# Output projection of a hybrid decoder layer: one fp32 product replaced by three products of hi and lo parts, with GpSimd making the weights' lo parts

## The chip, the cores and the metric

The kernel runs on one core of a Trainium2 chip. The metric is the device time of one execution in microseconds (us). Before the change the median of three runs is 924.68 us (923.85 to 926.58).

## What is computed

One decoder layer on 256 tokens of width 1024, batch 1, depth 1, float32 throughout. `c` is one vector that conditions the layer; everything between the input and the second normalization hangs on the modulation `mod`, six vectors of 1024:

```python
mod = jnp.einsum('bd,de->be', jax.nn.silu(c), w_ada[l]) + b_ada[l]
sh1, sc1, g1, sh2, sc2, g2 = jnp.split(mod[:, None, :], N_MOD, axis=-1)
h = rmsnorm(x, norm1_g[l]) * (1.0 + sc1) + sh1
proj = jnp.einsum('bsd,de->bse', h, w_in[l])
q, k, v, u = jnp.split(proj, [A, 2 * A, 3 * A], axis=-1)
attn = dilated_attention(q.reshape(B, S, N_HEADS, HEAD_DIM),
                         k.reshape(B, S, N_HEADS, HEAD_DIM),
                         v.reshape(B, S, N_HEADS, HEAD_DIM)).reshape(B, S, A)
pool = multiscale_pool(u, pool_w[l], pool_scale[l])
mixed = jnp.einsum('bse,ed->bsd', jnp.concatenate([attn, pool], axis=-1), w_out[l])
x = x + g1 * mixed
h2 = rmsnorm(x, norm2_g[l]) * (1.0 + sc2) + sh2
x = x + g2 * peer_ffn(h2, peer_wq[l], peer_subkeys[l], peer_u[l], peer_v[l])
return rmsnorm(x, final_g)
```

Attention has 8 heads of 64, the pooling mixer 4 groups of 128 channels. `peer_ffn` scores 16384 experts by product keys, takes the best 16 of each of 8 heads, and adds up their gated outputs. `mixed` is the output projection that the change touches: a 256 x 1024 by 1024 x 1024 product.

## The kernel before

Everything is held transposed, channels on the 128 partitions and the 256 tokens along the row, so that a 1024-channel quantity is eight blocks `k`. The program is written in order by hand, and each engine works through its own instructions in that order.

**Weights in two parts.** Most products are made in float32r, which the kernel feeds with two parts of each number: `hi`, a rounded copy made by ScalarE (ACT), and `lo`, what the rounding left, a subtraction made by VectorE (DVE). A product of two such numbers is then three matmuls, hi·hi, hi·lo and lo·hi. The input projection (lines 283 to 346), the query projection and the first expert product (`mm3`, lines 549 to 559) and the second expert product (`mmv`, line 973) are of this kind. The output projection is not: `out_proj` (lines 440 to 445) multiplies a block of `w_out` as it was loaded with a block of `cat`, both plain float32.

**The modulation.** Each of the vectors is made in eight blocks: `ada_dot` (line 195) is one DVE instruction that multiplies a 128 x 1025 block of `w_ada` with `silc`, the silu of `c` spread over all partitions, and adds up along the row. `ada_step` (line 202) does one block, frees its buffer, and for the scales (`SC1`, `SC2`) adds one small instruction (line 207). SC1 and SH1 are made during the input projection; the 24 blocks of G1, SC2 and SH2 (the list `rest`) are spread over the attention and the output projection by calls of `ada_steps(n)`. G2 is made much later.

**The stage around the change** (lines 349 to 492). `cat` has eight blocks: 0 to 3 are pairs of attention heads, 4 to 7 are the pooling groups. `pool_sums`, `pool_means` and `pool_mix` make blocks 4 to 7. For a pair of heads `p`, `s1` makes scores (PE), `s2d` adds the bias and finds the maxima (DVE, one operand from PSUM, line 397), `s2a` takes exponentials (ACT), `s3` normalizes, `s4` transposes (PE) and evacuates (ACT, line 425), and `s5` multiplies with the values (PE) and evacuates into `cat` (ACT, line 438). Between these stand `out_proj(0)` to `out_proj(6)`, in the order of blocks 4, 5, 6, 7, 0, 1, 2, 3; they accumulate into four banks of PSUM. `out_proj(7)` (line 530) closes them.

**What follows.** The loop at line 531 makes `x2 = xt + G1 * mixed` in eight DVE steps (line 532), with a square (ACT, line 535) and two times two small matmuls for the row sums (PE, line 537) each. DVE reaches line 532 only after the 23 modulation steps that stand ahead of it. Then come transposes (line 523), the reciprocal root, `h2h` and `h2l` (lines 578 and 593), the first three query products (line 571), and from there two long streams of 512 KB weight blocks to the end.

**Loads.** All of them go through SP's queue in one fixed order. `Loads` hands out a load when its kind has a free buffer in the program's order: kind `ada` has 7 buffers (blocks of `w_ada`), kind `big` has 8 (halves of blocks of `w_in`, later the blocks of `w_out`), kind `raw` has 3. On the chip a load waits in SP's queue until the buffer's last reader is done, and all loads behind it wait too. The order after the input projection's loads is set by the numbers of line 164: six blocks of `w_ada`, then blocks of `w_out` with two of `w_ada` between them:

```python
    for k, n in zip((4, 5, 6, 7, 0, 1, 2, 3, None), (6, 0, 0, 2, 2, 2, 2, 2, 8)):
        for _ in range(n):
            ada_load(*next(todo))
        if k is not None:
            load("big", ("wo", k), prep, [P, D], w_out[k], 8)
```

Of the kernel before, what the change touches and what calls it, by code (L numbers as in the profile page):

```python
# [29 lines left out]
PN1, PN2, PPS = 0, 8, 16  # L30
# [57 lines left out]
def _body(ctx, tc, xT, c, w_ada, cols, w_in, pool_w, w_out, peer_wq, subkeys, peer_u, peer_v, final_g,  # L88
          band, invw, iota_n, iota_k, out):
    nc = tc.nc  # L90
# [6 lines left out]
    colt = persist.tile([P, 20], F32, name="colt")  # L97
    ada = persist.tile([P, 48], F32, name="ada")
# [6 lines left out]
    h2h = persist.tile([P, KD, T], F32R, name="h2h")  # L105
    h2l = persist.tile([P, KD, T], F32R, name="h2l")

    pre = ExitStack()
    prep = pre.enter_context(tc.tile_pool(name="prep", bufs=1))

    NQ = 16
    ld = Loads()
    ld.pool("const", 99)

    def load(key, name, pool, shape, src, bufs):
        ld.free.setdefault(key, bufs)

        def go():
            t = pool.tile(shape, F32, name=key, bufs=bufs)
            nc.sync.dma_start(t, src)  # L120
            return t

        ld.add(key, name, go)

    def const(tile_, src):
        ld.add("const", None, lambda: nc.sync.dma_start(tile_, src))
# [22 lines left out]
        nc.sync.dma_start(xt[:, a:b, :], xT[:, a:b, :])  # L149
    nc.scalar.dma_start(colt, cols)  # L150

    def ada_load(v, k):
        load("ada", ("ada", v, k), prep, [P, D + 1], w_ada[v, k], 7)

    for k in range(KD):
        ada_load(SC1, k)
        ada_load(SH1, k)
        for j in ((0, 1) if k < KD - 1 else (1, 0)):
            load("big", (f"w{j}", k), prep, [P, D], w_in[k, :, j * D:(j + 1) * D], 8)
    const(invt, invw.to_broadcast([P, 4 * TOPK]).rearrange("p (g t) -> p g t", g=4))  # L160
    const(pwt, pool_w)
    rest = [(G1, k) for k in range(KD)] + [(v, k) for k in range(KD) for v in (SC2, SH2)]
    todo = iter(rest)
    for k, n in zip((4, 5, 6, 7, 0, 1, 2, 3, None), (6, 0, 0, 2, 2, 2, 2, 2, 8)):
        for _ in range(n):
            ada_load(*next(todo))
        if k is not None:
            load("big", ("wo", k), prep, [P, D], w_out[k], 8)
    streams = [peer_wq[i] for i in range(16)] + [peer_u[i] for i in range(NK)] + [peer_v[i] for i in range(NK)]
    LAST = 5  # L170
    early = {40 + 10 * j: NQ + 2 * NK - 3 + j for j in range(3)}
# [29 lines left out]

    def ada_step(v, k):
        ada_dot(v, k, ld.get(("ada", v, k)), junk, silc)
        ld.done("ada")
        if v in (SC1, SC2):
            g = (PN1 if v == SC1 else PN2) + k
            nc.vector.scalar_tensor_tensor(acol(v, k), acol(v, k), 1.0, colt[:, g:g + 1],
                                           op0=ALU.add, op1=ALU.mult)
# [46 lines left out]
    for k in ks:  # L255
        for tb in range(2):
            nc.tensor.matmul(banks[7][:, 0, tb:tb + 1], lhsT=sq[:, k, tb * P:(tb + 1) * P], rhs=ones[:, 0:1],
                             start=(k == ks[0] and tb == 0), stop=(k == ks[-1]), skip_group_check=True)
# [24 lines left out]
    for k in range(KD):  # L283
# [7 lines left out]
        t = prepa.tile([P, T], F32, name="t", bufs=2)  # L291
# [37 lines left out]
        else:  # L329
            for m in (8, 9, 10, 11):  # L330
                for n in range(3):
                    mm(m, n)
                if m % 2:
                    j = m // 2 - 4
# [13 lines left out]

    pra.close()
    prepb = pre.enter_context(tc.tile_pool(name="prepb", bufs=1))  # L350
    cat = prepb.tile([P, KD, T], F32, name="cat")
    def ada_steps(n):
        for _ in range(min(n, len(rest))):
            ada_step(*rest.pop(0))
# [5 lines left out]
    def pool_sums(ns):  # L360
        for n in ns:
            sh = 1 << n
            a = ss[-1]
            b = pool2 if n == 2 else sq[:, (0, 4, 0, 7)[n]:(4, 7, 0, 8)[n]]
            off = 0 if n == 0 else 1
            nc.vector.tensor_add(b[:, :, sh:T], a[:, off:, sh:T], a[:, off:, 0:T - sh])
            nc.vector.tensor_copy(b[:, :, 0:sh], a[:, off:, 0:sh])
            ss.append(b)
# [13 lines left out]
    def pool_mix():  # L382
        o = [att_bank(), att_bank()]
        for g in range(4):
            nc.tensor.matmul(o[g // 2][:, g % 2 * T:(g % 2 + 1) * T], lhsT=pwt[:, g, :], rhs=pooled[g],
                             start=True, stop=True)
        for g in range(4):
            nc.scalar.activation(cat[:, 4 + g, :], o[g // 2][:, g % 2 * T:(g % 2 + 1) * T], AF.Copy,
                                 scale=colt[:, PPS + g:PPS + g + 1])

    def s2d(p):
        for h in (2 * p, 2 * p + 1):
# [16 lines left out]
    def s3(p):  # L409
        for h in (2 * p, 2 * p + 1):  # L410
            s, mx = H[h]["s"], H[h]["mx"]
            nc.vector.reciprocal(mx[:, 4:6], mx[:, 2:4])
            for tb, cs in ((0, slice(0, P)), (1, slice(P, 384))):
                if p == 0:
                    nc.vector.tensor_scalar(s[:, cs], s[:, cs], mx[:, 4 + tb:5 + tb], None, op0=ALU.mult)
                else:
                    nc.scalar.activation(s[:, cs], s[:, cs], AF.Copy, scale=mx[:, 4 + tb:5 + tb])

    def s4(p):
        for h in (2 * p, 2 * p + 1):  # L420
            pt = att_bank()
            for i in range(3):
                nc.tensor.transpose(pt[:, i * P:(i + 1) * P], H[h]["s"][:, i * P:(i + 1) * P], ident)
            eT = prepb.tile([P, 384], F32, name="eT", bufs=3)
            nc.scalar.activation(eT, pt[:, 0:384], AF.Copy)
            H[h]["eT"] = eT

    def s5(p):
        o = att_bank()
        for j in range(2):  # L430
            h = 2 * p + j
            r = slice(j * HD, (j + 1) * HD)
            hs = slice(h * HD, (h + 1) * HD)
            eT = H[h]["eT"]
            nc.tensor.matmul(o[r, 0:T], lhsT=vn[:, 0, hs], rhs=eT[:, 0:T], start=True, stop=True)
            nc.tensor.matmul(o[r, P:T], lhsT=vn[:, 1, hs], rhs=eT[:, T:384], start=False, stop=True,
                             skip_group_check=True)
        nc.scalar.activation(cat[:, p, :], o[:, 0:T], AF.Copy)

    def out_proj(n, ms=range(KD)):  # L440
        k = (4, 5, 6, 7, 0, 1, 2, 3)[n]
        w = ld.ready[("wo", k)]
        for m in ms:
            nc.tensor.matmul(ob[m // 2][:, m % 2, :], lhsT=w[:, m * P:(m + 1) * P], rhs=cat[:, k, :],  # L444
                             start=(n == 0 and m % 2 == 0), stop=(n == 7), skip_group_check=True)

    def s2(p):
        s2d(p)
        s2a(p)

    ob = banks[0:4]
    ada_steps(1)
    pool_sums((0, 1, 2, 3))
    s1(1)
    s2(0)
# [75 lines left out]
    for m in range(KD):  # L531
# [31 lines left out]
    def q_bank(n):  # L563
        return psum[:, 1 + n % 3, 0:T]
# [10 lines left out]
    for k in range(KD + 3):  # L575
# [15 lines left out]
        if 2 <= k < KD + 2:  # L591
            j = k - 2
# [297 lines left out]
    for n in range(3, NQ + NK):  # L890
# [72 lines left out]
    for k in range(KD):  # L963
        b = 50 + 9 * k
# [24 lines left out]
    for i in range(NK):  # L989
        n = NQ + NK + i  # L990
# [147 lines left out]
```

## Time and profile before

| | us |
|---|---|
| median of three runs | 924.68 |
| profiled execution | 927.4 |
| its span | 925.6 |
| PE (TensorE matmul) busy | 911.3 (98%) |
| DVE busy | 691.4 (75%) |
| ACT busy | 455.7 (49%) |
| POOL (GpSimd) busy | 8.8 (1%), 18 instructions |

The profile is one execution. The span runs from its first to its last instruction; the 1.8 us between span and time lie around it. Busy shares are averages over stages of different kinds, and a busy PE is not PE at its peak, since the ends of its matmuls are modelled. So the stage of the change is read by itself: it lies at 62 to 107 us of the span, and what a change in it is worth is read from what ends last there.

### The profile page before, as it was taken

The page shows a single profiled execution, that of the slowest core. Times are in us where ns is not written, and L with a number is a line of the kernel's source. Part 1 is how long each engine was busy: PE and PEld are TensorE (multiplying, and loading weights), DVE is VectorE, ACT ScalarE, POOL GpSimd, SP SyncE. Part 2 cuts the span into 40 slices and gives each one's busy share as a digit, 9 for nine tenths or more (in the row PEclk, how much of TensorE's full clock was granted, in tenths as well). Part 3 has the DMA queues.
Part 4 walks back from the last instruction along what each step waited for, and adds up shares of the span by engine and source line. Part 5 has one row for each costly group of instructions (what it writes and reads, how often), then busy time and mean ns, then how long its engine had stood idle before and what let it go on. Part 6 is the DMA issues. An engine that isn't in the chain of part 4 may idle for free.

```text
span 925.6 us, 15909 instructions
## 1 busy us (share of the span) xinstructions
PE 911.3 (98%) x6279; PEld 829.7 (90%) x6279; DVE 691.4 (75%) x1285; ACT 455.7 (49%) x656; POOL 8.8 (1%) x18
## 2 busy tenths in 40 slices
PE   9999989999999999999999999999999999999996
PEld 7987889999999999999999998888878888888885
DVE  6999769899989778888888966555556666566665
ACT  4456355545554555454444445444446554444542
POOL 0000000000000000000000000000000000000001
PEclk9999999999999999999999999999999999999999
DMA  9987734456665555555555556666676776766651
GB/s 342 408 321 287 270 121 153 160 184 189 188 192 183 163 166 172 163 162 169 172 161 167 165 173 199 189 195 190 219 236 222 237 231 216 209 217 212 183 180 47
DMA packets 52061, 185.40 MB, mean 200 GB/s; under 512 B 6033, under 2 KB 6545, under 8 KB 51986
## 3 DMA queue, kind: packets, MB, share of 16 engines
q1 hardware_dynamic: 50402, 179.12, 58.9%
q0 software_dynamic: 1440, 5.25, 1.9%
q8 instruction: 49, 0.80, 0.4%
q14 instruction: 26, 0.21, 0.1%
q10 hardware_dynamic: 144, 0.01, 0.0%
HBM read 183.31 MB, written 1.05 MB: 199 GB/s over the span
## 4 chain that ended last, share of the span: by engine, by line
PE 90%; DVE 4%; ACT 2%; DMA 2%; issue 1%; ACTq 0%; DVEq 0%
PE psum L979 34%; PE psum L554 14%; PE psum L558 14%; PE psum L555 14%; PE psum L444 3%; DMA raw<-in_peer_v_dram 2%; PE psum L785 2%; PE psum L786 2%; DVE wlo L303 1%; PE psum L571 1%; DVE junk L196 1%; PE psum L835 1%; PE psum L236 1%; ACT whi L300 1%; ACT hi L504 1%
## 5 line engine op out<-in xcount | busy, mean ns | idle before, releaser
L509 DVE TENSOR_TENSOR lo<-raw,hi 128x1024 fp32r<-128x1024 f32 x269 | 328.8, 1224 | 204.6 <-ACT hi L504 203.8
L504 ACT ACTIVATE hi<-raw 128x1024 fp32r<-128x1024 f32 x269 | 285.1, 1060 | 317.1 <-PE psum L979 157.4
L554 PE MATMUL psum<-h2h,hi 128*128 128x256 f32 x1128 | 272.7, 283 | 0.4 <-ACT q L826 0.4
L555 PE MATMUL psum<-h2l,hi 128*128 128x256 f32 x1128 | 269.0, 280 | 0.0
L554 PEld LDWEIGHTS psum<-h2h,hi 128*128 128x128 f32 x1128 | 213.2, 189 | 0.6 <-ACT q L826 0.6
L555 PEld LDWEIGHTS psum<-h2l,hi 128*128 128x128 f32 x1128 | 212.9, 189 | 0.0
L558 PE MATMUL psum<-h2h,lo 128*128 128x256 f32 x1128 | 154.1, 280 | 0.0
L558 PEld LDWEIGHTS psum<-h2h,lo 128*128 128x128 f32 x1128 | 141.3, 189 | 0.0
L979 PE MATMUL psum<-hi,h2h 128*128 128x512 f32 x486 | 132.5, 393 | 0.7 <-ACT hi L504 0.7
L979 PE MATMUL psum<-lo,h2h 128*128 128x512 f32 x486 | 131.6, 391 | 0.0
L979 PE MATMUL psum<-hi,h2l 128*128 128x512 f32 x486 | 131.3, 390 | 0.0
L979 PEld LDWEIGHTS psum<-hi,h2l 128*128 128x128 f32 x486 | 91.3, 188 | 20.0
L979 PEld LDWEIGHTS psum<-lo,h2h 128*128 128x128 f32 x486 | 91.4, 188 | 19.7
L979 PEld LDWEIGHTS psum<-hi,h2h 128*128 128x128 f32 x486 | 90.6, 188 | 20.4 <-ACT hi L504 1.5
L196 DVE SCALAR_TENSOR_TENSOR junk<-ada,silc 128x1025 f32<-128x1025 f32 x40 | 48.9, 1223 | 0.7 <-DMA ada<-in_w_ada_dram 0.4
L804 ACT ACTIVATE a<-psum 128x256 f32<-128x256 f32 (+22 forms) x54 | 16.7, 352 | 60.5 <-DVE a L801 55.1
L886 DVE TENSOR_TENSOR h2l<-a,h2h 128x1024 fp32r<-128x1024 f32 x31 | 37.8, 1219 | 0.0
L785 PE MATMUL psum<-ah,ohb 128*128 128x128 f16 x256 | 33.1, 220 | 0.0
L786 PE MATMUL psum<-al,ohb 128*128 128x128 f16 x256 | 32.7, 218 | 0.0
L882 ACT ACTIVATE h2h<-a 128x1024 fp32r<-128x1024 f32 x31 | 32.4, 1044 | 0.0
L444 PE MATMUL psum<-cat,big 128*128 128x256 f32 x128 | 28.9, 383 | 0.0
L444 PEld LDWEIGHTS psum<-cat,big 128*128 128x128 f32 x128 | 24.0, 190 | 3.8 <-issue 0.8
(227 smaller groups left out, 809.8 us busy)
## 6 DMA issues: line engine op xcount, KB each, us to landing
raw<-in_peer_u_dram SPq DMA_DIRECT2D x128, 512.0 KB, 3.5
raw<-in_peer_v_dram SPq DMA_DIRECT2D x128, 512.0 KB, 4.3
ada<-in_w_ada_dram SPq DMA_DIRECT2D x40, 512.5 KB, 7.7
big<-in_w_in_dram SPq DMA_DIRECT2D x16, 512.0 KB, 10.2
raw<-in_peer_wq_dram SPq DMA_DIRECT2D x16, 512.0 KB, 3.5
a<-in_w_ada_dram POOLq DMA_DIRECT2D x8, 512.5 KB, 5.0
big<-in_w_out_dram SPq DMA_DIRECT2D x8, 512.0 KB, 6.5
out_dram<-a SPq DMA_DIRECT2D x4, 256.0 KB, 2.3
```

Source lines behind the costliest of these rows:

```text
L196: nc.vector.scalar_tensor_tensor(jk, blk, 1.0, sil, op0=ALU.mult, op1=ALU.mult, accum_out=ada[:, v * 8 + k:v * 8 + k + 1])
L444: nc.tensor.matmul(ob[m // 2][:, m % 2, :], lhsT=w[:, m * P:(m + 1) * P], rhs=cat[:, k, :], start=(n == 0 and m % 2 == 0), stop=(n == 7), ...
L504: nc.scalar.activation(hi, raw, AF.Copy)
L509: nc.vector.tensor_sub(lo, raw, hi.bitcast(F32))
L554: nc.tensor.matmul(o, lhsT=hi[:, cs], rhs=h2h[:, k, :], start=(k == 0), stop=False, skip_group_check=True)
L555: nc.tensor.matmul(o, lhsT=hi[:, cs], rhs=h2l[:, k, :], start=False, stop=False, skip_group_check=True)
L558: nc.tensor.matmul(o, lhsT=lo[:, cs], rhs=h2h[:, k, :], start=False, stop=(k == KD - 1), skip_group_check=True)
L785: nc.tensor.matmul(o[:, t, :], lhsT=b[:, pr, :, e], rhs=ah[:, pr, :, e], start=True, stop=False)
L786: nc.tensor.matmul(o[:, t, :], lhsT=b[:, pr, :, e], rhs=al[:, pr, :, e], start=False, stop=True)
L882: nc.scalar.activation(hi, a, AF.Copy)
L886: nc.vector.tensor_sub(lo, a, hi.bitcast(F32))
L979: nc.tensor.matmul(ycols(tb, cs) if o is None else o, lhsT=a[:, i % 4, tb * P:(tb + 1) * P], rhs=b[:, cs], start=st, stop=sp, skip_group_c ...
```

## The change

The output projection becomes three float32r products, as elsewhere in the kernel. For that, `w_out` and `cat` are taken apart:

- `wo_split(n)`: ACT makes `hi` of a block of `w_out`, GpSimd makes `lo` by a 128 x 1024 subtraction. Eight calls are spread over the stage. The parts stand in `h2h` (not yet in use) for n = 0, 3, 6, and in two pairs of buffers named "hi" and "lo" for the others.
- `cat_put(k, ...)`: ACT evacuates a block of `cat` twice, once as plain float32 (`t`) and once rounded (`cath`), and GpSimd subtracts the two (128 x 256) into `catl`, which stands in `h2l` (not yet in use).
- `out_proj(n)`: 24 matmuls where there were 8; all hi·hi and hi·lo first, the lo·hi behind them.
- Buffers of kind `big` are one column wider, so that they can hold a block of `w_ada`. Five of the 24 blocks are loaded into them, as soon as the input projection frees them, and the order of loads is a new string (capital B: a block of `w_ada` into `big`; a: into `ada`; a digit: a block of `w_out`).

```diff
+    slot_of = {}
+    def ada_load(v, k, key="ada"):
+        slot_of[v, k] = key
+        load(key, ("ada", v, k), prep, [P, D + 1], w_ada[v, k], 7 if key == "ada" else 8)
...
+    KO = (4, 5, 6, 7, 0, 1, 2, 3)
+    for what in "BBBBaaB0aa12aaaaa3a4a5a6a7aaaaaa":
+        if what in "aB":
+            ada_load(*next(todo), "ada" if what == "a" else "big")
+        else:
+            load("big", ("wo", KO[int(what)]), prep, [P, D + 1], w_out[KO[int(what)]], 8)
...
+    cath = prepb.tile([P, KD, T], F32R, name="cat")
+    catl = h2l
+    def cat_put(k, o, scale=1.0):
+        t = prepb.tile([P, T], F32, name="t", bufs=4)
+        nc.scalar.activation(t, o, AF.Copy, scale=scale)
+        nc.scalar.activation(cath[:, k, :], o, AF.Copy, scale=scale)
+        nc.gpsimd.tensor_sub(catl[:, k, :], t, cath[:, k, :].bitcast(F32))
+    def two(*names):
+        return [prepb.tile([P, D], F32R, name=x, bufs=2) for x in names]
+    WO = {}
+    def wo_split(n):
+        if n % 3 == 0:
+            hi, lo = (h2h[:, 4 * j:4 * j + 4, :].rearrange("p k t -> p (k t)") for j in range(2))
+        else:
+            hi, lo = two("hi", "hi") if n % 3 == 1 else two("lo", "lo")
+        w = ld.get(("wo", KO[n]))
+        nc.scalar.activation(hi, w, AF.Copy)
+        nc.gpsimd.tensor_sub(lo, w, hi.bitcast(F32))
+        ld.done("big")
+        WO[n] = hi, lo
...
     def out_proj(n, ms=range(KD)):
-        k = (4, 5, 6, 7, 0, 1, 2, 3)[n]
-        w = ld.ready[("wo", k)]
-        for m in ms:
-            nc.tensor.matmul(ob[m // 2][:, m % 2, :], lhsT=w[:, m * P:(m + 1) * P], rhs=cat[:, k, :],
-                             start=(n == 0 and m % 2 == 0), stop=(n == 7), skip_group_check=True)
+        hi, lo = WO[n]
+        ch, cl = cath[:, KO[n], :], catl[:, KO[n], :]
+        for part in range(2):
+            for m in ms:
+                for a, b in (((hi, ch), (hi, cl)), ((lo, ch),))[part]:
+                    nc.tensor.matmul(ob[m // 2][:, m % 2, :], lhsT=a[:, m * P:(m + 1) * P], rhs=b,
+                                     start=(n == 0 and a is hi and b is ch and m % 2 == 0),
+                                     stop=(n == 7 and part == 1), skip_group_check=True)
...
     ada_steps(1)
+    wo_split(0)
     pool_sums((0, 1, 2, 3))
...
     s2(2)
+    wo_split(1)
     out_proj(0)
     s5(0)
     s4(1)
+    wo_split(2)
...
     s3(3)
+    wo_split(3)
     ada_steps(2)
     s5(2)
+    wo_split(4)
     out_proj(2)
     s4(3)
+    wo_split(5)
...
     for n in range(4, 7):
         ada_steps(3)
+        if n < 6:
+            wo_split(n + 2)
         out_proj(n)
```

The order of instructions changes at two places that matter later. The first is GpSimd's whole program. Before, after the identity matrix (lines 197 and 199 of a helper), there is nothing until the loads for G2 late in the kernel:

```order
masks.py:197 MEMSET ident 128x128
masks.py:199 ISA
masks.py:199 AFFINE_SELECT ident<-ident 128x128
L951 DMA a_1265<-in_c_dram 128x1024
L933 DMA a_1265<-in_w_ada_dram 128x1025 x3
```

Now sixteen subtractions stand between them; 128x1024 rows are lo parts of `w_out` (into the second half of `h2h`, or the second buffer of "hi" or "lo"), 128x256 rows are `catl`, in `h2l`:

```order
masks.py:199 AFFINE_SELECT ident<-ident 128x128
L379 TENSOR_TENSOR h2h<-big,h2h 128x1024
L365 TENSOR_TENSOR h2l<-t,cat 128x256 x4
L379 TENSOR_TENSOR hi<-big,hi 128x1024
L365 TENSOR_TENSOR h2l<-t,cat 128x256
L379 TENSOR_TENSOR lo<-big,lo 128x1024
L365 TENSOR_TENSOR h2l<-t,cat 128x256
L379 TENSOR_TENSOR h2h<-big,h2h 128x1024
L365 TENSOR_TENSOR h2l<-t,cat 128x256
L379 TENSOR_TENSOR hi<-big,hi 128x1024
L379 TENSOR_TENSOR lo<-big,lo 128x1024
L365 TENSOR_TENSOR h2l<-t,cat 128x256
```

Two more 128x1024 rows follow, for n = 6 and 7, and then the loads for G2. Every one of these instructions reads two tensors in SBUF.

The second place is SP's queue behind the last loads of the input projection. Before:

```order
L126 DMA pwt<-in_pool_w_dram 128x512
L120 DMA ada<-in_w_ada_dram 128x1025 x6
L120 DMA big<-in_w_out_dram 128x1024 x3
L120 DMA ada<-in_w_ada_dram 128x1025 x2
L120 DMA big<-in_w_out_dram 128x1024
L120 DMA ada<-in_w_ada_dram 128x1025 x2
L120 DMA big<-in_w_out_dram 128x1024
```

Now:

```order
L126 DMA pwt<-in_pool_w_dram 128x512
L120 DMA big<-in_w_ada_dram 128x1025 x4
L120 DMA ada<-in_w_ada_dram 128x1025 x2
L120 DMA big<-in_w_ada_dram 128x1025
L120 DMA big<-in_w_out_dram 128x1024
L120 DMA ada<-in_w_ada_dram 128x1025 x2
L120 DMA big<-in_w_out_dram 128x1024 x2
L120 DMA ada<-in_w_ada_dram 128x1025 x5
L120 DMA big<-in_w_out_dram 128x1024
L120 DMA ada<-in_w_ada_dram 128x1025
L120 DMA big<-in_w_out_dram 128x1024
```

From the fourth block of `w_out` on, each stands behind one more block of `w_ada` that waits for a buffer of kind `ada`, which a modulation step on DVE frees.

## Rows read from the trace of the kernel before

**Rows 1.** Stretches: us; PE, PEld, DVE, ACT, POOL busy (instructions); PEclk; DMA share; GB/s

```profile
65.80:73.80 8.00, 6.28 (x34) 3.96 (x34) 7.75 (x39) 7.23 (x26) 0.00 (x0) 1.00 0.16 66
73.80:95.00 21.20, 20.95 (x123) 16.71 (x122) 19.61 (x53) 11.11 (x37) 0.00 (x0) 1.00 0.98 360
95.00:104.10 9.10, 9.10 (x46) 7.99 (x43) 8.86 (x18) 1.87 (x3) 0.00 (x0) 1.00 1.03 409
```

**Rows 2.** Timeline of DVE, 102 to 110 us: start us, us, line, operation

```profile
102.71 1.23 DVE L196 SCALAR_TENSOR_TENSOR junk<-ada,silc 128x1025 f32<-128x1025 f32 x1
103.86 0.08 DVE L196 DVE_READ_ACCUMULATOR junk<-ada,silc 128x1 f32 x1
103.98 0.16 DVE L207 SCALAR_TENSOR_TENSOR ada<-ada,colt 128x1 f32<-128x1 f32 x1
106.60 3.47 DVE L532 SCALAR_TENSOR_TENSOR xt<-psum,ada,xt 128x256 f32<-128x256 f32 x8 [2.46 <-PE psum L444]
```

**Rows 3.** Chain that ended last, in order of time: start us, us, what

```profile
73.83 3.65 PE psum L444 x16
...
95.14 14.01 PE psum L444 x64
109.15 3.46 PE psum L537 x32
112.61 2.92 PE psum L523 x16
...
132.09 0.94 PE psum L558 x8
```

**Rows 4.** Groups, whole span, of ACT and GpSimd: busy us, mean ns

```profile
L300 ACT ACTIVATE whi<-big 128x1024 fp32r<-128x1024 f32 x16 | 16.1, 1043 | 0.0
L388 ACT ACTIVATE cat<-psum,colt 128x256 f32<-128x256 f32 x4 | 1.5, 460 | 0.0
L438 ACT ACTIVATE cat<-psum 128x256 f32<-128x256 f32 x4 | 1.5, 379 | 6.5 <-PE psum L436 6.5
L1032 POOL TENSOR_TENSOR a<-a 128x512 f32<-128x512 f32 x2 | 2.6, 1292 | 69.4 <-DVE a L1020 68.7 <-DVE st L1028 0.6
```

**Rows 5.** Timeline of POOL at the kernel's end, then of DVE beside it

```profile
912.52 1.29 POOL L1032 TENSOR_TENSOR a<-a 128x512 f32<-128x512 f32 x1 [68.75 <-DVE a L1020]
914.44 1.29 POOL L1032 TENSOR_TENSOR a<-a 128x512 f32<-128x512 f32 x1 [0.63 <-DVE st L1028]
...
911.68 0.69 DVE L1020 TENSOR_TENSOR a<-a,x2nat 128x512 f32<-128x512 f32 x1
912.29 0.68 DVE L1019 TENSOR_TENSOR a<-psum,a 128x512 f32<-128x512 f32 x1
913.00 1.36 DVE L1020 TENSOR_TENSOR a<-a,x2nat 128x512 f32<-128x512 f32 x1
...
915.29 0.68 DVE L1019 TENSOR_TENSOR a<-psum,a 128x512 f32<-128x512 f32 x1
```

**Rows 6.** Timeline of ACT: end of the input projection, last squares

```profile
64.18 0.60 ACT L341 ACTIVATE kT<-psum 128x512 f32<-128x512 f32 x1
...
109.64 1.69 ACT L535 ACTIVATE t<-xt 128x256 f32<-128x256 f32 x4
```

**Rows 7.** Groups of DVE, 65.8 to 104.1 us: busy us, mean ns

```profile
L196 DVE SCALAR_TENSOR_TENSOR junk<-ada,silc 128x1025 f32<-128x1025 f32 x22 | 26.9, 1224 | 0.3
L397 DVE CUSTOM_DVE_ANT_0 biast<-biast,psum 128x128 f32<-128x128 f32 (+1 forms) x16 | 5.3, 352 | 1.1 <-PE psum L279 0.6
L378 DVE SCALAR_TENSOR_TENSOR x2nat<-x2nat,uT 128x240 f32<-128x240 f32 x3 | 1.2, 404 | 0.0
```

**Rows 8.** Stretches behind the stage (columns as in rows 1)

```profile
112.60:117.50 4.90, 3.79 (x20) 3.06 (x18) 2.37 (x9) 2.91 (x6) 0.00 (x0) 0.65 0.23 88
120.70:124.00 3.30, 3.30 (x18) 3.21 (x18) 3.30 (x10) 2.11 (x5) 0.00 (x0) 0.60 0.55 182
124.00:130.00 6.00, 5.64 (x49) 5.44 (x47) 2.31 (x4) 1.88 (x4) 0.00 (x0) 1.00 0.27 90
```

More of the change, by code (lines that the diff above doesn't have):

```diff
@@ L118, in go @@
         def go():
-            t = pool.tile(shape, F32, name=key, bufs=bufs)
+            t = pool.tile(shape, F32, name=key, bufs=bufs)[:, 0:src.shape[-1]]
             nc.sync.dma_start(t, src)
@@ L150, in _body @@
     nc.scalar.dma_start(colt, cols)
-    def ada_load(v, k):
-        load("ada", ("ada", v, k), prep, [P, D + 1], w_ada[v, k], 7)
+    slot_of = {}
+    def ada_load(v, k, key="ada"):
+        slot_of[v, k] = key
+        load(key, ("ada", v, k), prep, [P, D + 1], w_ada[v, k], 7 if key == "ada" else 8)
     for k in range(KD):
@@ L158, in _body @@
         for j in ((0, 1) if k < KD - 1 else (1, 0)):
-            load("big", (f"w{j}", k), prep, [P, D], w_in[k, :, j * D:(j + 1) * D], 8)
+            load("big", (f"w{j}", k), prep, [P, D + 1], w_in[k, :, j * D:(j + 1) * D], 8)
     const(invt, invw.to_broadcast([P, 4 * TOPK]).rearrange("p (g t) -> p g t", g=4))
@@ L163, in _body @@
     todo = iter(rest)
[L164 to L168, printed above, removed]
+    KO = (4, 5, 6, 7, 0, 1, 2, 3)
[4 more added lines that the diff above has]
+            load("big", ("wo", KO[int(what)]), prep, [P, D + 1], w_out[KO[int(what)]], 8)
+    assert not list(todo)
     streams = [peer_wq[i] for i in range(16)] + [peer_u[i] for i in range(NK)] + [peer_v[i] for i in range(NK)]
@@ L203, in ada_step @@
         ada_dot(v, k, ld.get(("ada", v, k)), junk, silc)
-        ld.done("ada")
+        ld.done(slot_of[v, k])
         if v in (SC1, SC2):
@@ L350, in _body @@
     prepb = pre.enter_context(tc.tile_pool(name="prepb", bufs=1))
-    cat = prepb.tile([P, KD, T], F32, name="cat")
+    cath = prepb.tile([P, KD, T], F32R, name="cat")
[18 more added lines that the diff above has]
+        WO[n] = hi, lo
     def ada_steps(n):
@@ L387, in pool_mix @@
         for g in range(4):
-            nc.scalar.activation(cat[:, 4 + g, :], o[g // 2][:, g % 2 * T:(g % 2 + 1) * T], AF.Copy,
-                                 scale=colt[:, PPS + g:PPS + g + 1])
+            cat_put(4 + g, o[g // 2][:, g % 2 * T:(g % 2 + 1) * T], colt[:, PPS + g:PPS + g + 1])
     def s2d(p):
@@ L437, in s5 @@
                              skip_group_check=True)
-        nc.scalar.activation(cat[:, p, :], o[:, 0:T], AF.Copy)
+        cat_put(p, o[:, 0:T])
     def out_proj(n, ms=range(KD)):
-        k = (4, 5, 6, 7, 0, 1, 2, 3)[n]
-        w = ld.ready[("wo", k)]
-        for m in ms:
-            nc.tensor.matmul(ob[m // 2][:, m % 2, :], lhsT=w[:, m * P:(m + 1) * P], rhs=cat[:, k, :],
-                             start=(n == 0 and m % 2 == 0), stop=(n == 7), skip_group_check=True)
+        hi, lo = WO[n]
[6 more added lines that the diff above has]
+                                     stop=(n == 7 and part == 1), skip_group_check=True)
     def s2(p):
```

## The prediction

> **What bounds the kernel now.** I read the stretches of the stage first. There PE is busy for 20.95 of 21.20 us and then all the time, and DVE for 19.61 of 21.20 and 8.86 of 9.10 [rows 1]: two engines are full, and it has to be settled which is late last. GpSimd does nothing, ACT is half free. The timeline of DVE answers it: the last modulation step ends at 104.1, then DVE is idle for 2.46 us until PE has the first pair of blocks of `out_proj(7)`, and the eight steps of line 532 start at 106.6 [rows 2]. I call this start S; everything behind it hangs on it. So PE ends last by 2.46 us and DVE is next. The chain in order of time shows the same from PE's side: 64 records of line 444 without a gap from 95.14 to 109.15, and right behind them the row sums, the transposes and the root's broadcast [rows 3]. A faster product alone can give back at S no more than DVE's 2.46 us of slack, wherever DVE doesn't become faster too. What the new work does to DVE is therefore the question.
>
> **Edits on PE.** One block of the projection is 16 records in 3.65 us, or 64 records in 14.01, so 3.5 us [rows 3]. Eight matmuls of the same 256 columns in float32r take 0.94 us [rows 3], so three products take 2.82. That is 0.7 us a block, 5.5 us in all. It is real, but only 2.46 us of it reach S by the paragraph above.
>
> **Edits on ACT.** Eight roundings of 128x1024 at 1.04 us, eight more evacuations at 0.38 to 0.46 [rows 4]: 8.3 + 3.3 = 11.6 us on an engine that is busy for 7.23 + 11.11 + 1.87 = 20.2 of 38.3 us [rows 1]. The four evacuations of the pooling groups become eight, 1.5 us longer, and the next scores on PE wait for them; I count that at nothing, because DVE, which sets S below, has modulation steps to do in that time. If that cover were gone, it would cost up to 1.5 us.
>
> **Edits on SP's queue.** Five blocks of `w_ada` come earlier, into buffers that were idle, so the first modulation steps are never short of data. The blocks of `w_out` for n = 3 to 7 now stand behind loads that wait for modulation steps. As long as these run on time the blocks are there on time. When DVE falls behind, they come later, and GpSimd's work with them: DVE's lateness feeds itself. The wider buffers cost nothing: a block stays at 512 KB.
>
> **Edits on GpSimd.** Sixteen subtractions, eight of 128x1024, eight of 128x256. No row shows these sizes. The nearest is a 128x512 product of two SBUF tensors, 1.29 us twice [rows 4, 5], 2.52 ns for a column; by it 1024 columns take 2.58 us and 256 take 0.65, together 8 x 2.58 + 8 x 0.65 = 25.8 us. There is room for that in the 38.3 us, and PE waits for none of it as long as it runs free.
>
> But it doesn't run free. At 912.52 to 913.81 GpSimd works on two SBUF tensors. The DVE instruction of line 1020 that also reads two SBUF tensors starts at 913.00 and takes 1.36 us, where the same instruction just before takes 0.69 [rows 5]; GpSimd's own 1.29 is not longer than in its second run. The DVE instructions of line 1019, which have one operand in PSUM, take 0.68 beside either of GpSimd's runs [rows 5]. I read it so: while GpSimd reads two SBUF operands, a DVE instruction with two SBUF operands stands still, 0.67 us here, which is about what was left of GpSimd's run. [...]
>
> In the stage DVE's work is just of that kind. From 65.8 us, when ACT can have rounded the first block of `w_out` (kT's evacuation ends at 64.8 [rows 6], one rounding is 1.04), to 104.1 the 22 modulation products read a block and `silc`, both in SBUF: 26.9 us [rows 7]. The pooling subtractions of lines 374, 378 and 380 are twelve small ones of the same kind, three of them 1.2 us [rows 7]; I count 2.7 for all. So 29.6 of these 38.3 us are work that can't go on beside GpSimd, and 8.7 us are other work or idle: line 397 with its operand in PSUM (5.3 us busy [rows 7]), small reciprocals, waits. So DVE ends its steps between
>
> - 104.1 + 25.8 - 8.7 = 121.2, if GpSimd's work fills all 8.7 us, and
> - 104.1 + 25.8 = 129.9, if it fills none of them.
>
> I take 122, near the lower end: GpSimd's next operands are mostly ready when DVE stands off, so little of the 8.7 is lost. It doesn't matter much which of the two engines wins: what one gains the other loses, and line 532 needs both, DVE through the order of its instructions and GpSimd through the lo parts of `out_proj(7)`. PE is done earlier: `out_proj(7)` has its lo part before DVE's last steps, since GpSimd's list ends before DVE's. So S moves from 106.6 to 122, by 15.4 us.
>
> GpSimd's price is the weak term. [...] I stay with the row.
>
> **Behind S.** Before, the row sums on PE could only start at 109.0 behind `out_proj(7)`, and ended at 112.6, S + 6.0. Now PE is free and each sum follows its square: ACT's last square ends at S + 4.7 as before (109.64 + 1.69 against 106.6 [rows 6]), the last four small matmuls take 4 x 0.11 [rows 3], so S + 5.2: 0.8 us gained. Against it stands the clock. In the trace it is 1.00 through the stage [rows 1] and falls only after the row sums of one column each: 0.65 and 0.60 of full speed in two stretches, and back at 1.00 from 124, when the query products run [rows 8]. [...] I take 1.4, nearer to the low end because ACT's squares set the pace of the sums. Together +0.6.
>
> **The sum.** 15.4 + 0.6 = 16.0 us later. The profiled execution has a span of 925.6 and a time of 927.4, so 943.4 by it; it lies 2.7 us above the median of the runs, 924.68, and against that the forecast is **940.7 us**, 1.7% slower. From about 130 us on nothing in the program differs, PE has no slack there, and the delay stays.
>
> **Rivals.**
>
> *The operands don't collide (faster).* The whole reading rests on one doubled row, and line 1020 is another operation than the modulation product, which also adds up along its row. If the latter doesn't stand still, GpSimd's 25.8 us are hidden in 38.3, and DVE's 104.1 sets S: 2.5 us earlier, and 0.8 from the row sums: 3.3 less, 921.4. It decides on whether line 196 stays at 1.22 us beside GpSimd. Against it stands that 1.36 fits GpSimd's end so well. Chance 0.15.
>
> *They collide by half.* If both go on at a lower rate when they meet, DVE loses half of 25.8 - 8.7, so 8.6; S is at 112.7, 6 us later: 931. A half rate would have made the 0.69 about 1.1, not 1.36 [rows 5]. Chance 0.13.
>
> *DVE always wins, and GpSimd starves.* The modulation steps follow each other so closely that GpSimd may get in only where DVE stands off. Then DVE ends near 104, and from there GpSimd has the lo parts from n = 3 on and two blocks of `catl` to do: 5 x 2.58 + 2 x 0.65 = 14.2, to 118.3, and the last products end a us later: S near 119.5, PE at its lower clock before it. That is 13 to 16 us, 938 to 941, the same time with another face: line 532 waits for PE, not for DVE. Chance 0.14.
>
> *GpSimd is slower than its row.* A column at 3.3 ns, because the result is float32r or because its turn comes late, gives 34 us for the sixteen and S near 130: 949. Chance 0.09.
>
> That the three products could fail to be cheaper than the one is excluded by their rows (2.82 against 3.5 us a block).
>
> **How the numbers follow.** The forecast itself has a chance of 0.49. A measurement of this kernel tells about 0.3%, 2.8 us, from no change. The likeliest case's own range, from the two ends of the cover and of the clock, is 938 to 949. The range that is to hold the time 8 times in 10 takes in the half collision at 931 with some room, and the slow GpSimd at 949: **928 to 950**; left out are the faster rival and the tails. Faster by over 0.3%: most of the first rival, 0.11. Within: its rest and the low tail of the half collision, 0.06. Slower: 0.83.
>
> **What would show it.** Right: line 196 has many instances near 2.5 to 3.8 us or with idle time ahead of them, sixteen subtractions on POOL from about 66 to 112 us, line 532's successor starts near 122 with DVE late and PE idle before it, the granted clock is down there. The three products take 2.8 us a block where nothing is waited for. Wrong: the modulation products stay at 1.22 us while POOL is busy; or POOL's subtractions take well under 2.3 us; or S waits for PE with DVE idle (the starving rival).

## The result, and the profile after

| | before | after |
|---|---|---|
| median, us | 925.63 (4 runs, 923.85 to 926.89) | 941.06 (4 runs, 940.08 to 942.15) |
| ratio after to before, 95% interval | | 1.0168 [1.015, 1.0186] |
| profiled execution, its span, us | 927.4, 925.6 | 940.4, 938.6 |

The changed kernel is 1.7% slower: 941.06 us, where 940.7 was forecast. Its stretches, with the columns of [rows 1]: us; PE, PEld, DVE, ACT, POOL busy; PEclk; DMA share; GB/s.

```profile
73.80:95.00 21.20, 20.05 (x146) 17.48 (x146) 18.79 (x44) 16.86 (x48) 14.89 (x9) 0.92 0.44 149
95.00:104.10 9.10, 8.71 (x69) 7.76 (x68) 9.00 (x9) 5.64 (x10) 9.00 (x5) 1.00 1.00 399
104.10:113.90 9.80, 6.19 (x48) 5.58 (x46) 9.66 (x11) 0.48 (x1) 7.08 (x3) 1.00 0.64 177
113.90:120.20 6.30, 0.00 (x0) 0.00 (x0) 6.13 (x13) 0.00 (x0) 0.00 (x0) 0.81 0.93 362
121.00:126.00 5.00, 4.82 (x23) 4.82 (x23) 4.71 (x10) 3.73 (x9) 0.00 (x0) 0.50 0.08 23
```

DVE is full to the end, and PE has nothing at all to do in the last 6.3 us before the residual (the sum `x2` of line 573, line 532 before): the engine that ended last before is now the one that waits. But DVE's instructions are no more than they were: 9 in 9.10 us from 95.0, where [rows 1] had 18. The timeline of DVE shows why (start us, us, line, operation; the small rows that read the sums out are left out):

```profile
93.15 2.26 DVE L213 SCALAR_TENSOR_TENSOR ada<-ada,colt 128x1 f32<-128x1 f32 x1
...
95.33 1.83 DVE L202 SCALAR_TENSOR_TENSOR junk<-ada,silc 128x1025 f32<-128x1025 f32 x1
...
97.20 3.29 DVE L202 SCALAR_TENSOR_TENSOR junk<-ada,silc 128x1025 f32<-128x1025 f32 x1
...
107.75 1.22 DVE L202 SCALAR_TENSOR_TENSOR junk<-ada,silc 128x1025 f32<-128x1025 f32 x1
...
109.01 3.25 DVE L202 SCALAR_TENSOR_TENSOR junk<-ada,silc 128x1025 f32<-128x1025 f32 x1
...
112.38 1.22 DVE L202 SCALAR_TENSOR_TENSOR junk<-ada,silc 128x1025 f32<-128x1025 f32 x1
...
120.20 1.26 DVE L573 SCALAR_TENSOR_TENSOR xt<-psum,ada,xt 128x256 f32<-128x256 f32 x3
```

And beside it POOL's, with its first, some of the middle and its last subtractions:

```profile
65.81 2.37 POOL L379 TENSOR_TENSOR h2h<-big,h2h 128x1024 fp32r<-128x1024 f32 x1 [64.50 <-PE psum L285]
...
84.07 2.41 POOL L379 TENSOR_TENSOR lo<-big,lo 128x1024 fp32r<-128x1024 f32 x1
...
91.92 3.47 POOL L379 TENSOR_TENSOR h2h<-big,h2h 128x1024 fp32r<-128x1024 f32 x1 [3.78 <-ACT h2h L378]
95.36 0.72 POOL L365 TENSOR_TENSOR h2l<-t,cat 128x256 fp32r<-128x256 f32 x1
96.04 3.37 POOL L379 TENSOR_TENSOR hi<-big,hi 128x1024 fp32r<-128x1024 f32 x1
...
107.78 3.40 POOL L379 TENSOR_TENSOR hi<-big,hi 128x1024 fp32r<-128x1024 f32 x1
```

Read the two together. The subtraction of 96.04 is on record for 3.37 us, where one that starts ahead of DVE takes 2.37 or 2.41: it first waits for the product of 95.33, which ends at 97.16. Then it runs 2.3 us, to 99.41. The product of 97.20 stands still that long and ends 1.08 us later. The last pair does the same: subtraction to 111.18, product from 109.01 to 112.26. From there POOL is done, and every product takes 1.22 again. Even the tiny instruction of line 213, one column wide (line 207 before, 0.16 us in [rows 2]), is held for the length of a subtraction: 2.26 us at 93.15, until the subtraction of 91.92 ends.

The groups of DVE from 65.8 to 120.2 sum it up (busy us, mean ns):

```profile
L202 DVE SCALAR_TENSOR_TENSOR junk<-ada,silc 128x1025 f32<-128x1025 f32 x18 | 27.5, 1528 | 0.3
L202 DVE SCALAR_TENSOR_TENSOR junk<-big,silc 128x1025 f32<-128x1025 f32 x4 | 7.5, 1874 | 0.0
L213 DVE SCALAR_TENSOR_TENSOR ada<-ada,colt 128x1 f32<-128x1 f32 x8 | 7.5, 935 | 0.3
```

Against 1.22 and 0.16 each, that is 35.0 - 22 x 1.22 = 8.2 us in the products and 7.5 - 8 x 0.16 = 6.2 in the tiny ones. With 0.8 in the pooling (two instructions of line 405) DVE stood still for 15.2 us. The eight subtractions of 1024 columns take some 2.39 us each where they don't wait, the eight of 256 take 0.72, together 24.9.

The chain in order of time, beside [rows 3]:

```profile
76.14 4.56 PE psum L476 x24
...
118.86 1.25 DVE junk L202 x2
120.20 0.49 DVE xt L573
120.71 0.42 ACT t L576
121.18 6.99 PE psum L578 x32
128.17 3.45 PE psum L564 x16
131.62 0.45 PE psum L232 x2
```

The modulation on DVE has taken the place of `out_proj` as the last thing ahead of S. S is 120.20; it was 106.60 [rows 2]. Behind it the row sums take 6.99 us instead of 3.46, at a clock of 0.50; before it was 1.00 there. The first product of the MLP comes at 145.25, 25.05 us behind S; before it came at 129.94, 23.34 behind. From there on the two programs are the same, yet that stretch takes 795.7 us before and 793.4 after, and 792.9 to 797.7 in the twelve profiled executions of this document. So of the 15.3 us by which the MLP begins later the two spans show 13.0, and traces are compared below only as far as the MLP.

One thing to know ahead of the runs: single executions differ in when the stage begins. The last evacuation of kT is at 64.18 before [rows 6] and within 0.03 us of that in most runs, but 1.6 to 1.8 us earlier in three of them (e3, e7, e10). S is counted from this mark below, as if it stood at 64.18 each time. Ratios are to the kernel before as it ran in the same session, where its median lay between 925.6 and 927.5.

### The profile page after: what moved, and what is told of

It is laid out like the page before. It is cut to its first block, busy times and chain, and to the rows that moved or that the text cites. A ratio compares the mean times of both kernels' runs of the same rounds, so it can differ in the third digit from the quotient of the medians.

```text
span 938.6 us, 16077 instructions
## 1 busy us (share of the span) xinstructions
PE 911.4 (97%) x6343; PEld 832.9 (89%) x6343; DVE 705.8 (75%) x1285; ACT 466.0 (50%) x672; POOL 42.8 (5%) x34
## 4 chain that ended last, share of the span: by engine, by line
PE 88%; DVE 7%; issue 2%; ACT 2%; ACTq 0%; DVEq 0%
PE psum L1020 37%; PE psum L595 14%; PE psum L596 14%; PE psum L599 14%; DVE junk L202 4%; PE psum L826 2%; PE psum L827 2%; DVE wlo L309 1%; PE psum L612 1%; PE psum L876 1%; PE psum L578 1%; PE psum L242 1%; ACT whi L306 1%; PE psum L476 0%; PE psum L323 0%
## 5 line engine op out<-in xcount | busy, mean ns | idle before, releaser
L1020 PEld LDWEIGHTS psum<-hi,h2h 128*128 128x128 f32 x486 | 90.7, 188 | 19.1
L842 DVE SCALAR_TENSOR_TENSOR a<-psum,a 128x768 f32<-128x768 f32 (+31 forms) x42 | 27.2, 668 | 0.0
L853 ACT ACTIVATE a<-psum 128x512 f32<-128x512 f32 (+30 forms) x59 | 26.5, 449 | 0.0
```

The costliest lines, as they stand in the source:

```text
L842: nc.vector.scalar_tensor_tensor(a[:, :, ts], oT[:, r, :], 1.0 / GSC, a[:, :, ts], op0=ALU.mult, op1=ALU.mult)
L1020: nc.tensor.matmul(ycols(tb, cs) if o is None else o, lhsT=a[:, i % 4, tb * P:(tb + 1) * P], rhs=b[:, cs], start=st, stop=sp, skip_group_c ...
```

## Experiments

**e1: GpSimd doesn't read.** The lo parts are zeros that GpSimd writes; ACT's work, the loads and the products on PE stay. A fill has no operands, so it also waits for no load and no rounding, and it is shorter: five of the sixteen are done at the start of the kernel, the other eleven fall between 66 and 101 us.

```diff
-        nc.gpsimd.tensor_sub(catl[:, k, :], t, cath[:, k, :].bitcast(F32))
+        nc.gpsimd.memset(catl[:, k, :].bitcast(F32), 0.0)
...
-        nc.gpsimd.tensor_sub(lo, w, hi.bitcast(F32))
+        nc.gpsimd.memset(lo.bitcast(F32), 0.0)
```

> The sixteen subtractions of GpSimd become fills with zero of the same places (the lo parts of w_out and of cat are left at zero); order, waits, loads, ACT and PE are unchanged. GpSimd then reads nothing from SBUF. Theory (a DVE instruction with two SBUF inputs stands still while GpSimd reads SBUF): no modulation product is above 1.25 us, line 532's successor starts at 103 to 105 in place of 120.2, 921 to 924 us, 17 to 20 below the changed kernel. Rival (the lateness comes from the new chain of order, loads, roundings and products): the start stays at 112 to 120, 933 to 941 us.

Measured: 929.07, ratio 1.0029 [1.0016, 1.0042]. The products in the groups of DVE, then three rows of its timeline with what DVE waited for ahead of them, then a fill on POOL and the product beside it:

```profile
L202 DVE SCALAR_TENSOR_TENSOR junk<-ada,silc 128x1025 f32<-128x1025 f32 x19 | 23.3, 1224 | 2.5 <-DMA ada<-in_w_ada_dram 2.3
L202 DVE SCALAR_TENSOR_TENSOR junk<-big,silc 128x1025 f32<-128x1025 f32 x4 | 4.9, 1218 | 0.0
```

```profile
83.15 0.29 DVE L427 CUSTOM_DVE_ANT_0 biast<-biast,psum 128x128 f32<-128x128 f32 x1 [2.56 <-PE psum L285]
...
103.23 1.23 DVE L202 SCALAR_TENSOR_TENSOR junk<-ada,silc 128x1025 f32<-128x1025 f32 x1 [2.27 <-DMA ada<-in_w_ada_dram]
...
109.80 3.22 DVE L573 SCALAR_TENSOR_TENSOR xt<-psum,ada,xt 128x256 f32<-128x256 f32 x8
```

```profile
87.18 0.95 POOL L379 MEMSET hi<- 128x1024 f32 x1 [5.21 <-PE psum L476]
...
87.96 1.23 DVE L202 SCALAR_TENSOR_TENSOR junk<-ada,silc 128x1025 f32<-128x1025 f32 x1
```

All stretching is gone, and with it about 12 of the 15 us. The fills (0.95 us for 1024 columns) ran on the same engine in the same stage, and no product was longer than 1.23 for it. So the stretching comes from the subtractions on GpSimd, and the "no collision" rival falls; that it is their reading and not their length, e8 shows.

But the expected time was missed: S is at 109.8, where 103 to 105 was expected, and the kernel is not faster than before even so. Something else costs 5.7 us against 104.1. The rows name it: 2.56 us for scores that come late on PE, 2.27 for a block of `w_ada`, and 1.8 in three waits for ACT, together 6.6, where DVE stood idle for 1.1 ahead of line 397 before, 0.6 of it for PE [rows 7].

**e8: GpSimd reads one operand.** Copies of the same sizes take the place of the subtractions. The lo parts are then whole copies of the blocks, not what the rounding left, and the copies wait for no rounding.

```diff
-        nc.gpsimd.tensor_sub(catl[:, k, :], t, cath[:, k, :].bitcast(F32))
+        nc.gpsimd.tensor_copy(catl[:, k, :], t)
...
-        nc.gpsimd.tensor_sub(lo, w, hi.bitcast(F32))
+        nc.gpsimd.tensor_copy(lo, w)
```

> GpSimd copies the blocks in place of subtracting (lo parts become the rounded whole, so the output is another): one SBUF operand in place of two. Theory (any GpSimd instruction that reads SBUF holds up a two-input DVE instruction for its own length): modulation products of 1.5 to 2.2 us are seen, as long as GpSimd's copies last (about 1 us each), start at 112 to 116, 931 to 936 us. Rival (only GpSimd's own second operand collides): all products at 1.22, as the first experiment, 929 us.

Measured: 935.40, ratio 1.0087 [1.0057, 1.0118], S at 110.75. Groups of DVE:

```profile
L202 DVE SCALAR_TENSOR_TENSOR junk<-ada,silc 128x1025 f32<-128x1025 f32 x19 | 24.5, 1287 | 0.3
L213 DVE SCALAR_TENSOR_TENSOR ada<-ada,colt 128x1 f32<-128x1 f32 x8 | 3.5, 434 | 0.3
```

Line 213 averages 434 ns, not 160, and single products reach 1.94. A GpSimd instruction with one SBUF operand holds DVE as well, only for less: its copies take 1.04 and 0.40 us. They are hardly longer than the fills of e1 (0.95 and 0.31), beside which nothing stretched: what holds DVE is the reading. The rival (only a second operand of GpSimd collides) falls. The time is as expected, but its place is not: S was to lie at 112 to 116. Of the 4.6 us between the two profiled spans (932.0, and 927.4 in e1) S carries 1.0 and the way from S to the MLP 1.1 (25.4 us, 24.3 in e1); the rest lies in the MLP and behind it, where the programs don't differ and executions do, and stays unexplained.

**e9: twice the subtractions.** Each subtraction of a `w_out` block is done twice.

```diff
         nc.gpsimd.tensor_sub(lo, w, hi.bitcast(F32))
+        nc.gpsimd.tensor_sub(lo, w, hi.bitcast(F32))
```

> The changed kernel, with each of the eight subtractions of a w_out block done twice on GpSimd, the same result written again. Theory (each GpSimd instruction with two SBUF operands takes its whole time from VectorE, wherever VectorE has operations of that kind to do): eight more subtractions of 2.4 us are 19 us of GpSimd work; some of it falls into waits of VectorE as now (about a third), so the residual starts 12 to 19 us later than in the changed kernel, at 132 to 139, and the time is 953 to 960. Rival 1 (GpSimd's work lies beside VectorE's list, and what the change costs comes from waits for ScalarE and TensorE): the residual stays at 120 to 122, the time at 941 to 943. Rival 2 (GpSimd becomes late, and TensorE waits for its lo parts): the residual moves too, but VectorE's products keep their lengths and the idle time before the residual grows.

Measured: 961.8, ratio 1.0348 [1.0304, 1.0392], S at 136.6. DVE, then POOL, in one stretch:

```profile
122.29 1.21 DVE L202 SCALAR_TENSOR_TENSOR junk<-ada,silc 128x1025 f32<-128x1025 f32 x1
...
123.54 3.27 DVE L202 SCALAR_TENSOR_TENSOR junk<-ada,silc 128x1025 f32<-128x1025 f32 x1
...
126.86 2.17 DVE L213 SCALAR_TENSOR_TENSOR ada<-ada,colt 128x1 f32<-128x1 f32 x1
```

```profile
122.31 3.42 POOL L379 TENSOR_TENSOR h2h<-big,h2h 128x1024 fp32r<-128x1024 f32 x1
125.81 3.20 POOL L380 TENSOR_TENSOR h2h<-big,h2h 128x1024 fp32r<-128x1024 f32 x1
```

At the end, PE and then DVE:

```profile
135.72 1.01 PE L477 MATMUL psum<-cat,hi 128*128 128x256 f32 x3 [3.72 <-POOL hi L380]
...
136.56 0.88 DVE L574 SCALAR_TENSOR_TENSOR xt<-psum,ada,xt 128x256 f32<-128x256 f32 x2 [0.87 <-PE psum L477]
```

The two engines take turns: product, subtraction, product, subtraction, and each record holds the wait for the other. DVE stands still for 32 us (15.0 and 1.0 in the two groups of products, 13.0 in line 213, 3.0 in the pooling), 17 more than in the changed kernel, for 19.1 us of added GpSimd work. S moves by 16.4, inside what the theory expected; the products don't keep their lengths, as rivals 1 and 2 would have it. Rival 2 has a share at the very end all the same: GpSimd's list now ends with DVE's, at 135.7, PE waits 3.7 us for each of the last two lo parts, and 0.87 of the 16.4 us is DVE waiting for PE. The time is 1.8 us above the range: PE stands still for longer now, its clock is 0.77 from 65.8 to 136.6, and the way from S to the MLP takes 28.4 us instead of 25.05.

**e5: no reading, other loads.** As e1, and an order of loads in which no `w_out` block stands behind a load that waits for a modulation step of this stage; all blocks of `w_ada` are in buffers of kind `ada`.

```diff
-    for what in "BBBBaaB0aa12aaaaa3a4a5a6a7aaaaaa":
+    for what in "aa01aa23aa45a67aaaaaaaaaaaaaaaaa":
```

> Fills in place of the subtractions as in the first experiment (lo parts of w_out and cat left at zero), and a third order of loads: all eight blocks of w_out go into the wide buffers in pairs as the input projection frees them, the blocks of w_ada all into their own seven. Theory: of the 5.7 us by which the first experiment's start (109.80) lay behind 104.1, the 2.27 us wait of DVE for a block of w_ada belongs to the order of loads and goes; the waits for PE at its lower clock and for ACT's double evacuations (4.3 us) stay: start at 107 to 108, 926 to 928 us. Rival (all of the remainder is loads): start at 104, 923 us.

Measured: 926.87, ratio 0.9992 [0.9971, 1.0013], S at 106.8. The wait for the block of `w_ada` is gone, the waits for PE (2.5) and ACT (1.2) stay. With neither collision nor that wait the three products end in the time of the kernel before, not below it.

**e6: the changed kernel with those loads.** The same line of the diff, with the subtractions as they are.

> The changed kernel with that third order of loads and nothing else. Theory (DVE stands still for 15 us whenever GpSimd does its 24.9 us, early or late): GpSimd no longer idles for blocks of w_out, but the sum of standing still is the same 13 to 17 us, 938 to 942 us. Rival (the coupling of the loads costs several us by itself): 930 to 936 us.

Measured: 942.92, ratio 1.0153 [1.0112, 1.0194], S at 119.98; DVE stands still for 15.1 us, within the expected 13 to 17, and the time is 0.9 above the range. The rival falls. What was worth 3 us of S without the collision is worth nothing with it. That DVE's lateness feeds itself through SP's queue, as the prediction feared, isn't what costs.

**e3: the new loads alone.** The kernel before, with the change's buffers and order of loads.

```diff
-    for k, n in zip((4, 5, 6, 7, 0, 1, 2, 3, None), (6, 0, 0, 2, 2, 2, 2, 2, 8)):
...
+    for what in "BBBBaaB0aa12aaaaa3a4a5a6a7aaaaaa":
```

> The kernel before with the new order of loads and the wider buffers alone; the output projection is the old one. Theory: the stage was not short of data before, 0 to 1 us of difference, 925 to 927 us. Rival (blocks of w_out behind waiting blocks of w_ada hold up the projection): PE waits for loads from the fourth block on, 928 to 935 us.

Measured: 924.94, ratio 0.9987 [0.997, 1.0004]: no difference. Its trace has 2.8 us of DVE waiting for `w_ada` too, and S at 108.4 from the common mark; the medians don't show it. It also has what e1 has, scores that come late: two stretches (columns as in [rows 1]), `out_proj(0)` on PE, and the scores' reader on DVE:

```profile
68.40:72.20 3.80, 2.70 (x15) 1.74 (x14) 3.69 (x15) 3.80 (x14) 0.00 (x0) 0.95 0.07 28
72.20:76.00 3.80, 3.80 (x11) 2.87 (x11) 3.70 (x13) 2.97 (x12) 0.00 (x0) 0.60 0.00 0
```

```profile
72.54 5.02 PE L450 MATMUL psum<-cat,big 128*128 128x256 f32 x16
...
80.06 0.29 DVE L403 CUSTOM_DVE_ANT_0 biast<-biast,psum 128x128 f32<-128x128 f32 x1 [2.29 <-PE psum L285]
```

`out_proj(0)` is the old one here, and took 3.65 us in the trace before [rows 3].

**e2: the lo parts on DVE.** Both subtractions move to DVE, at the same places of the program.

```diff
-        nc.gpsimd.tensor_sub(catl[:, k, :], t, cath[:, k, :].bitcast(F32))
+        nc.vector.tensor_sub(catl[:, k, :], t, cath[:, k, :].bitcast(F32))
...
-        nc.gpsimd.tensor_sub(lo, w, hi.bitcast(F32))
+        nc.vector.tensor_sub(lo, w, hi.bitcast(F32))
```

> The same sixteen subtractions on DVE, GpSimd idle. Theory: the 15.2 us of standing still go, and DVE gets 8 x 1.15 + 8 x 0.35 = 12.0 us of work of its own: the start of line 532's successor at 116 to 118, 937 to 939 us. Rival (GpSimd's work is late, not in the way): DVE's 12 us take the place of nothing, 950 us or more.

Measured: 950.70, ratio 1.0272 [1.024, 1.0304], S at 130.6; a miss. The subtractions themselves are 1.22 and 0.42 us, 13.2 in all, less than the 15.2 that DVE lost to GpSimd. But two rows of DVE's timeline show what else they bring:

```profile
101.81 1.23 DVE L379 TENSOR_TENSOR h2h<-big,h2h 128x1024 fp32r<-128x1024 f32 x1 [2.95 <-ACT h2h L378]
...
110.12 1.23 DVE L379 TENSOR_TENSOR lo<-big,lo 128x1024 fp32r<-128x1024 f32 x1 [3.13 <-ACT lo L378]
```

Each subtraction stands in DVE's queue right behind ACT's rounding, and holds up the modulation steps that need nothing of it: 15.7 us of idle time in all. So the time lies in the rival's range, but not for the rival's reason. The chain goes through two waits for `w_out` (5.32 and 4.41 us), whose loads wait for those steps.

**e7: the same with the loads of e5.**

> The sixteen subtractions on DVE as in the second experiment, with the third order of loads. Theory: the second experiment's 950.7 us come from DVE standing in its own queue behind roundings that wait for blocks of w_out, whose loads wait for DVE's next steps (15.7 us idle for ACT); with the blocks there early, only DVE's own 12 us and some 3 us of waits are left: start at 118 to 121, 938 to 942 us. Rival (it is DVE's own work): 948 us or more.

Measured: 949.83, ratio 1.0242 [1.0201, 1.0282], S at 127.1 from the common mark; a miss again. 12.2 us of waiting for ACT stay (6.1 of them for the roundings of n = 0 and 3), beside 13.3 us of subtractions. The time lies in the rival's range, and DVE's own work is about half of the cause; the place in the queue is the other half, and the loads are little of it. DVE subtractions put where their operands are long there weren't tried.

**e4: PE kept busy before the row sums.** 32 useless products (64 records) behind `out_proj(7)`.

```diff
         out_proj(7, (m, m + 1))
+    keep_warm(32)
```

> The changed kernel with 32 small products more behind the last block of the projection, some 7 us of PE that nobody waits for, in the place where PE stands still from 113.9 to 121.2. Theory (the row sums take 6.99 us in place of 3.46 because PE meets them at its lower clock level): row sums end 2 to 3 us earlier relative to their start, 938 to 939 us. Rival (ACT's squares or DVE set that pace): no difference, 941 us.

Measured: 941.33, ratio 1.0157 [1.0127, 1.0188]. It decides nothing: in this execution the clock fell within `out_proj(7)` (0.63 from 110 to 116), the useless products lasted until 125.3, and the row sums, now 3.68 us, waited for them. They ended no earlier.

**e10: paced.** Small groups of useless products, each behind one modulation column.

```diff
+    columns = list(rest)
...
+    for v, k in columns[17:23]:
+        nc.tensor.matmul(banks[5][:, 0, 0:1], lhsT=ones, rhs=acol(v, k), start=True, stop=True)
+        keep_warm(4)
```

> The changed kernel, with products of no use on TensorE behind the last output projection block, one small group behind each of the last six modulation columns, so that TensorE goes on working until the residual starts without being late for it. Theory (the row sums of the second norm, 7.0 us beside 3.5 before, are late because the clock fell while TensorE stood idle for 7.3 us before them): the 32 row sums take 3.5 us again, the first product of the MLP begins 23 to 24 us behind the residual's start instead of 25, and the time is 939 to 940, 1 to 2 us below the changed kernel's. Rival (single executions differ by that much whatever TensorE does before): the time stays at 941 to 942, and the first product at 25 us behind the start even if the row sums are faster.

Measured: 942.43, ratio 1.0164 [1.0135, 1.0194]. PE's row sums:

```profile
119.75 1.84 PE L582 MATMUL psum<-ones,t 128*128 128x1 f32 x16
121.87 2.99 PE L582 MATMUL psum<-ones,t 128*128 128x1 f32 x16 [0.27 <-ACT t L580]
```

The clock was 1.00 up to the row sums, and their first half took 1.84 us; the second took 2.99, and from 121 to 126 the clock was 0.65. Before the change it was low right behind them, 0.65 from 112.6 [rows 8]. They took 5.1 us instead of 7.0, and the MLP began 24.4 us behind S, not 25.05. The 0.7 us don't show in the median, and the theory's 939 to 940 is missed: the rival holds, in that the time doesn't move.

## Why the prediction was right

**The bound was read right.** DVE's slack of 2.46 us was all that PE's gain could reach, and what the change does to DVE decided. The three products are cheaper, as worked out: `out_proj(2)` runs from 89.6 to 92.5 us, 2.9 for a block instead of 3.5. None of it shows: PE waits 4.0 us for GpSimd's lo parts on the way, is done at 113.9, and then waits 7.3 us for DVE.

**The collision is real, and is a full stop.** It was inferred from a single doubled row [rows 5]. After, instances of 3.25 and 3.29 us stand where 1.22 stood, e1 takes them away with fills, e8 brings part of them back with one operand read, and e9 adds 16.4 us to S for 19.1 us of work. "Half" would have made products of at most about 2.4 (2 x 1.22) and no halt of a whole subtraction in a one-column instruction. Neither does GpSimd starve: its list ends at 111.2, ahead of DVE's, because the two take turns.

**GpSimd's price** was 25.8 us by the row, and is 24.9. The difference of the two sizes here gives (2.39 - 0.72) us / 768 = 2.17 ns for a column, where the row had 2.52. The rest of the 0.72 us, some 0.17, comes on top in each of the sixteen, an estimate from these two sizes.

**Three terms were off, and their errors cancelled.** The forecast was a list that ends at 104.1 without the collision, and 17.9 us of standing still.

- *"ACT counted at nothing", and "the first modulation steps are never short of data".* Without collision S isn't 104.1 but 109.8 (e1): the rival "no collision", priced at 921.4, would have been 929. The largest piece is 2.56 us in which DVE waits for scores; the prediction had the evacuations ahead of these scores at nothing, and at 1.5 us at most. PE makes the scores behind `out_proj(0)`, whose 24 matmuls took 4.56 us in the changed kernel, at a clock of 0.66 from 76 to 81; in the trace before, the clock was 1.00 there. That is a term that the prediction didn't have. ACT's longer evacuations are not its cause alone: with them PE was busy for 2.18 us in the 3.80 from 70.0, where it was 2.70 before, but in e3, without them and again with 2.70 of 3.80, the clock fell to 0.60 at the same place, and DVE waited 2.29 us for the scores. What brings it down stays open, and so does how much of the 5.7 us belongs to the change.
- *"If it fills none of them … if it fills all 8.7".* Measured against e1, the collision costs 10.4 us at S. DVE stands still for 15.2, but some of that falls where it would have waited for PE, ACT or data anyway.
- *The tail*, forecast at +0.6, is +1.7: the row sums end at S + 8.0, where S + 5.2 and 1.4 for the clock were counted. No run shows the 1.4: after the change the row sums took 6.99 us at 0.50 instead of 3.46 at 1.00, and the transposes behind them 3.45 at 0.53 instead of 2.92 at 0.59.

Why the cancelling is not quite chance: work that excludes itself adds up, and waits of DVE can go by beneath it. The prediction's lower end is this sum: 104.1 + 25.8 - 8.7 is 65.8 + 29.6 + 25.8, and it doesn't hang on the waits in the list that ends at 104.1. From 65.8, 29.6 us of DVE work that can't run beside GpSimd and 24.9 of GpSimd's end at 120.3; S is 120.2. The same sum gives 139.4 for e9 (136.6 measured) and, with 8 x 1.04 + 8 x 0.40 = 11.5 us of copies, 106.9 at most for e8, below the 109.8 that the waits alone give (110.75 measured). So S is the later of two ends, the waits' and the sum's, within 3 us in these runs (that e9 ends ahead of its sum shows that some of the work does overlap); and e6 shows that mending the waits moves nothing while the sum is later. It is an account that fits these numbers; no run isolates it, and that the number came within 0.4 us of the median is luck.

Half of the last link stays open: why the kernel without collision (e5) only draws level. The cheaper products and the loads are there, and S is 106.8, as before. DVE is the bound then, with its waits of 2.5 us for PE and 1.2 for ACT; what would bring it to 104 was not tried. No version that was run is faster than the kernel before by more than the measurement can tell.

## What to carry to other kernels

Before giving GpSimd work "because it is idle", list what DVE does in that stretch: where it read two SBUF tensors here, most of GpSimd's SBUF-reading time was added to DVE's (15.2 of 24.9 us, and 17 of 19.1 more in e9), whatever the busy shares said; a subtraction that cost DVE 1.22 us when it made it itself cost it up to 2.3 of standing still when GpSimd made it. To tell a collision from a dependency, keep the instructions and take the reading away (a fill, which also drops the waits for operands; so put a copy of about the same length beside it), then double the work: the first must restore the lengths, the second must add up. And price the rivals' base as carefully as the forecast: a rival at 921 that would really have been 929 can make a right number out of two wrong terms.

## What was not expected of the hardware

- An instruction one column wide that does 0.16 us of work is held 2.2 us by a subtraction on GpSimd, and on record as busy: DVE's busy time goes from 691.4 to 705.8 us for the same 1285 instructions.
- GpSimd and DVE take turns (e9), in the records 3.2 to 3.5 us for a 2.39 us subtraction from 82 us on; neither starves the other, though DVE waited for other engines for only 0.5 us between 65.8 us and the end of its list.
- PE's clock fell to 0.66 within the attention (76 to 81 us) in the changed kernel, behind pauses of 0.5 to 1.1 us, and to 0.60 in e3 with PE busy for 2.70 of the 3.80 us ahead of it, as in the trace before, where it stayed at 1.00. It also fell in row sums of one column even when PE had been busy at 1.00 up to them (e10: 4.42 of the 4.50 us from 113.9 at 1.00, then 0.65 from 121 to 126).
